# An encoder layer on one core: the up projection by 1024 columns with tokens stationary, its results transposed, and another order in the last down blocks

## The chip, the cores and the metric

The kernel runs on one core of a Trainium2 chip. The time of a version is the device time of one execution in microseconds, and the median over runs is compared. In the views PE is the matrix engine (PEld its weight loads), DVE the vector engine, ACT the scalar engine, POOL the GpSimd engine and SP the engine that issues most DMAs. A matmul has a stationary side (at most 128 x 128, loaded first) and a moving side (at most 512 columns), and adds up in one of eight PSUM banks of 128 x 512 numbers.

## The reference

256 tokens, model width 2048, inner width 8192, all in float32:

```python
h = rms_norm(x, norm_mix_pre)
proj = h @ w_in                     # q, k, v of two attentions, two gates
...
mixed = g_a * (oa @ w_branch_a) + g_b * (on @ w_branch_b)
x = x + rms_norm(mixed @ w_out, norm_mix_post)
h = rms_norm(x, norm_mlp_pre)
u = square(relu(h @ w_up))          # 2048 -> 8192
x = x + rms_norm(u @ w_down, norm_mlp_post)
```

## The kernel before

**Products.** Every float32 operand is split into a high part in the matrix engine's own 32-bit format and the rest. A product is then three matmuls: high by high, high by rest, rest by high. Splitting a weight costs an ACT cast (the high part) and a DVE subtraction (the rest). Weights come as 1 MB tiles on SP's queue, three buffers of each kind in the pool `wp`.

**Two ways to lay out a projection.** In `wgroup` (L184) the weight is stationary and the activations move: for each 128 rows and 128 columns one matmul of 512 moving columns (the high parts of the 256 tokens, then their rests, L192) and one of 256 (weight rest by high parts, L193). Results come out with columns on partitions. Their two halves are added in `halves` (L252). In `agroup` (L221) and `wide_group` (L671) the tokens are stationary, 128 at a time, and the weight moves, 512 columns in each matmul. `wide_group` works on 1024 columns of the weight and takes its rows in eight pairs of 128. One pair is a 2 x 2 by 2 x 2 block product of 128 x 128 and 128 x 512 blocks: eight products of blocks, 24 matmuls (`eight`, L656), or seven products by Winograd's scheme, 21 matmuls (`seven`, L644). Seven products need sums of weight blocks (`pair_weights`, L602, lines L612 to L623), sums of activation blocks (`sums_of`, L693), four more PSUM banks and a recombination of five vector steps (`combine`, L662).

**The stages.** (1) q, k, v and the attentions, (2) the gates and the branch projections with `wide_group`, (3) the output projection with `agroup` in four groups of 512 columns (L896), (4) the normalised residual, transposed and split into eight tiles `h2T` by `residual_parts(t, c)` (L849; t is the half of the tokens, c a quarter of the columns), (5) the up projection (L993), (6) the down projection (L1050), (7) the final norm, residual and stores (`finish`, L1036).

**Up projection.** Sixteen groups of 512 columns with `wgroup`. The per-token scale of the norm is broadcast along the tokens by two small matmuls (`along_tokens`). `u_evac` adds the halves, applies relu and the scale, and squares. `act_sets` (L947) then makes what the down projection needs of these 512 columns: for an even group number four sums of blocks and the splits of blocks and sums, for an odd one the splits alone. They are written to DRAM (POOL's queue, L974). Two groups' sets stay on the chip.

**Down projection.** Two halves of 1024 output columns (g), each in eight blocks of four row pairs (`steps`, L1054). The sets of the next block are fetched back by `act_again` (L979), with DMAs issued on ACT's queue (L987). In each block two of the four pairs use seven products, in the first block of a half one. In the last block the pairs go seven, eight, seven, eight; after the second seven the recombination runs, and in the last pair each bank is finished and handed to `down_piece` (L1027: addition, square with row sum, gain). `finish(t)` runs when both banks of a token half are done.

**Buffers and order.** Most tiles live in a pool of 27 buffers of 4 KB per partition (`pages`); a second, small pool `mid` of five such buffers holds the splits of the weight sums. Scratch tiles of stages 1 and 3 to 5 come from a pool `tmp`. Each engine's queue is laid out by the framework's own scheduler, which may put a ready instruction ahead of one that stands earlier in the program; `issue_after` forbids that for a single instruction.

Of the kernel before, what the change touches and what calls it, by code (L numbers as in the profile page):

```python
# [38 lines left out]
def encoder_layer(ctx: ExitStack, tc: tile.TileContext, a, out):  # L39
# [559 lines left out]
    def wtile(tag, name):  # L599
        return wp.tile([P, 4, 512], F32R, tag=tag, name=name)  # L600

    def pair_weights(view, name, seven):  # L602


        raw = wp.tile([P, 4, 512], F32, tag="raw", name=f"{name}r")
        last_load[0] = nc.sync.dma_start(raw.rearrange("p (h b) c -> p h (b c)", h=2), view).ins
        h1, l1 = wtile("hi", f"{name}h"), wtile("lo", f"{name}l")
        if not seven:
            nc.scalar.copy(h1, raw)
            nc.vector.tensor_sub(l1, raw, h1.bitcast(F32))  # L610
# [3 lines left out]
        nc.vector.tensor_add(t[0], raw[:, 1:3], raw[:, 0:1].to_broadcast([P, 2, 512]))  # L614
        nc.vector.tensor_add(t[1][:, 0], t[0][:, 0], raw[:, 2])
        nc.vector.tensor_add(t[1][:, 1], t[1][:, 0], raw[:, 3])
        nc.vector.tensor_sub(l1[:, 1:4], raw[:, 1:4], h1[:, 1:4].bitcast(F32))
        h2, l2 = [], []
        for i in range(2):
            for part, n in ((h2, "eh"), (l2, "el")):  # L620
                part.append(mid.tile([P, 2, 512], F32R, tag="e", name=f"{name}{n}{i}"))
            nc.scalar.copy(h2[i], t[i])
            nc.vector.tensor_sub(l2[i], t[i], h2[i].bitcast(F32))  # L623
        return h1, l1, h2, l2
# [3 lines left out]
    class Products:  # L628

        def __init__(self, name, mm_banks, used=range(8)):
            self.ps = {i: bank(f"{name}{i}", i in mm_banks) for i in used}
            self.begun = set()

        def add(self, i, stat, w, blk, last=False):

            (sh, sl), (wh, wl) = stat, w
            nc.tensor.matmul(self.ps[i], sh, wh[:, blk], start=i not in self.begun, stop=False)  # L639
            self.begun.add(i)  # L640
            nc.tensor.matmul(self.ps[i], sh, wl[:, blk], start=False, stop=False)  # L641
            nc.tensor.matmul(self.ps[i], sl, wh[:, blk], start=False, stop=last)  # L642

        def seven(self, stat, w, last):  # L644

# [22 lines left out]
            nc.vector.tensor_sub(c12, self.ps[4], c12)  # L668
            nc.vector.tensor_sub(c22, self.ps[4], c21)

    def wide_group(name, kinds, view, stat7, stat8, mm_banks, z, piece, each=None):  # L671


        any7 = any(s for _, s in kinds)
        pr = Products(name, mm_banks, range(8) if any7 else (1, 2, 3, 7))
# [17 lines left out]
    def sums_of(p1, p2, name, hi=None, lo=None):  # L693

        a11, a21, a12, a22 = p1[:, :P], p1[:, P:], p2[:, :P], p2[:, P:]
        s = t2k(f"{name}s").rearrange("p a (b c) -> p (a b) c", b=2)
# [55 lines left out]
    for h in range(2):  # L752
        gate = []
        for br, gc in (("a", GA), ("b", GB)):
# [30 lines left out]
            if first_one:  # L785
                advance(99)
                temps.close()
                stage = ctx.enter_context(ExitStack())
                mid = stage.enter_context(tc.tile_pool(name="mid", bufs=5, reuse_waits="tile"))
# [22 lines left out]
        mixed.append(gate[0])  # L812
    for n in range(2):
        mixed_T(1, n)
    stage.close()
    temps = ctx.enter_context(ExitStack())
    tmp = temps.enter_context(tc.tile_pool(name="tmp", bufs=6, reuse_waits="tile"))


    def mstat(k, t):  # L820
# [20 lines left out]
    r2b = const.tile([P, T], F32, name="r2b")  # L841
    hT2 = [page([P, 2, 512], F32R, f"h2T{i}") for i in range(8)]

    def post_norm(t):
# [38 lines left out]
    def mlp_squares(t):  # L883
        for c in range(4):
            cs = slice((c % 2) * 512, (c % 2 + 1) * 512)
            j = junk512("jx").rearrange("p a b -> p (a b)")
# [9 lines left out]
    for cg in range(4):  # L896

        def y_evac(t, ps, cg=cg):
            j = junk512("jy").rearrange("p a b -> p (a b)")
# [9 lines left out]
    mlp_squares(0)  # L909
    tail = [residual_parts(1, 0)]  # L910
    after = {1: tail[0][1:]}


    def first_up_inner(k):
        if k == 1:
            tail.append(residual_parts(1, 1, tail[0][2]))
            after[2] = tail[-1][1:]
            return tail[-1][0]

    def first_up_chunk(ch):  # L920
        if 1 <= ch <= 2:
            residual_parts(0, ch + 1)
            tail.append(residual_parts(1, ch + 1, tail[-1][2]))
        if ch == 2:
            with tc.issue_after(tail[-1][1]):
                mlp_squares(1)
            for t in range(2):
                mlp_scale(t)

    first_up = dict(  # L930
        after=after,
        hook=first_up_chunk,
        inner=first_up_inner,
        mid=partial(along_tokens, r2, r2b, "r2b"),
        k_first=True,
    )

# [52 lines left out]
        return out  # L990

    sets = {}
    for cg in range(NG):  # L993
        u = page([P, 4, T], F32, f"u{cg}")

        def u_evac(b, ps, u=u):
            s = halves(ps, "up")
            nc.vector.scalar_tensor_tensor(s, s, 0.0, r2b, op0=ALU.max, op1=ALU.mult)  # L998
# [8 lines left out]
    temps.close()  # L1007
    mid = ctx.enter_context(tc.tile_pool(name="mid2", bufs=5, reuse_waits="tile"))
    wd = a["w_down"].rearrange("(g h j p) c -> p h g j c", h=2, j=2, p=P)

    def dstat7(sets, j, n):
# [38 lines left out]
    for g in range(2):  # L1050
        pr = Products(f"p{g}", (1, 2, 3, 7))
        for bi, b in enumerate(blocks[g]):
            if bi == 0:
# [3 lines left out]
            end = bi == len(blocks[g]) - 1  # L1057
            for n, (cg, j, seven) in enumerate(steps):
                w = pair_weights(wd[:, :, cg, j, g * 1024 : (g + 1) * 1024], f"d{g}{cg}{j}", seven)
                if n == 0:  # L1060
                    for c in range(2):
                        if not end:
# [10 lines left out]
                if g == 1 and bi == 6:  # L1073
                    gain(0, n // 2, n % 2)
                if seven:
                    pr.seven(partial(dstat7, sets[g, cg], j), w, end and n == 2)
                    if end and n == 2:
# [65 lines left out]
```

## Time and profile before

| | |
|---|---|
| median of three runs | 1376.75 us (1376.13 to 1379.43) |
| profiled execution, device time | 1378.19 us |
| its span in the trace | 1376.4 us |
| up projection, first matmul to last | 663.8 to 1026.4 us |
| PE, DVE, ACT busy | 98%, 72%, 52% |
| mean granted PE clock | 0.993 |

The rows of the profile have the form: line, engine, operation, written tile <- read tiles, shapes, count, busy time, mean duration in ns, idle time before, and what ended it. In a timeline the first number is the start, the second the length; "x8" groups several instructions. Durations of matmuls overlap, so the time that one costs is read from the distances between starts.

### The profile page before, as it was taken

The numbers are of one execution on the slowest core, as the hardware profiler recorded it, in microseconds if no ns is written. First come the engines' busy times: TensorE is split into PE (matmuls) and PEld (weight loads), VectorE is DVE, ScalarE is ACT, GpSimd is POOL, SyncE is SP. The second block draws the span as 40 slices with busy tenths as digits, with TensorE's granted clock in tenths as the row PEclk, the third lists the DMA queues.
The fourth block names the chain that finished last, engine by engine and source line by source line (L and its number), as shares of the span: only waits on it lengthen the run. The fifth ranks groups of instructions, "written<-read, shape, count | busy, mean of one in ns | idle before, by whom it ended". The sixth has DMA issues, their size and how long they took to land.

```text
span 1376.4 us, 17243 instructions
## 1 busy us (share of the span) xinstructions
PE 1345.8 (98%) x6771; PEld 1141.3 (83%) x6771; DVE 997.7 (72%) x1245; ACT 709.7 (52%) x939; POOL 34.3 (2%) x67
## 2 busy tenths in 40 slices
PE   7999999999999999999899999999999999999995
PEld 6888888888888888888788888888887888888884
DVE  6868866677857886654767666666667888888886
ACT  7455555544644554444755555555554455555552
POOL 0000000000000000000000000000000000000000
PEclk9999999999999999999999999999999999999998
DMA  8684745564555665666477777877779989699982
GB/s 304 204 229 159 207 154 183 174 186 154 198 191 191 214 205 190 225 237 198 138 257 248 248 245 255 267 244 239 267 253 350 346 337 355 239 355 353 354 337 87
DMA packets 131633, 329.63 MB, mean 239 GB/s; under 512 B 17120, under 2 KB 18400, under 8 KB 131552
## 3 DMA queue, kind: packets, MB, share of 16 engines
q1 hardware_dynamic: 113168, 264.03, 57.5%
q10 hardware_dynamic: 12240, 40.91, 7.7%
q0 software_dynamic: 6144, 23.60, 4.2%
q8 instruction: 53, 0.87, 0.3%
q14 instruction: 28, 0.23, 0.0%
HBM read 302.81 MB, written 27.51 MB: 240 GB/s over the span
## 4 chain that ended last, share of the span: by engine, by line
PE 92%; DVE 3%; DMA 3%; ACT 1%; issue 1%; ACTq 0%; POOL 0%; SPq 0%; DVEq 0%; POOLq 0%
PE u_p L192 17%; PE u_p L193 9%; PE p L641 6%; PE p L642 6%; PE p L639 6%; PE qa_p L192 2%; PE ka_p L192 2%; PE qn_p L192 2%; PE kn_p L192 2%; PE ga L639 2%; PE y_p L232 2%; PE ga L641 2%; PE ga L642 2%; PE y_p L230 2%; PE y_p L231 2%; PE gb L639 2%
## 5 line engine op out<-in xcount | busy, mean ns | idle before, releaser
L192 PE MATMUL u_p<-h2T,u_h 128*128 128x512 f32 x1024 | 359.5, 397 | 1.0 <-DVE h2T L870 1.0
L193 PE MATMUL u_p<-h2T,u_l 128*128 128x256 f32 x1024 | 284.2, 280 | 0.0
L192 PEld LDWEIGHTS u_p<-h2T,u_h 128*128 128x128 f32 x1024 | 191.7, 188 | 45.8 <-DVE h2T L870 1.2
L117 DVE TENSOR_TENSOR u_l<-u_w,u_h 128x1024 fp32r<-128x1024 f32 x128 | 151.1, 1222 | 89.7 <-ACT u_h L116 88.4
L193 PEld LDWEIGHTS u_p<-h2T,u_l 128*128 128x128 f32 x1024 | 193.6, 189 | 1.3
L116 ACT CAST u_h<-u_w 128x1024 fp32r<-128x1024 f32 x128 | 128.0, 1048 | 94.0 <-PE u_p L192 83.5
L117 DVE TENSOR_TENSOR y_l<-y_w,y_h 128x1024 fp32r<-128x1024 f32 x32 | 37.9, 1222 | 30.9 <-ACT y_h L116 30.9
L116 ACT CAST y_h<-y_w 128x1024 fp32r<-128x1024 f32 x32 | 32.1, 1051 | 40.9 <-PE y_p L232 32.5
L230 PE MATMUL y_p<-y_h,mh 128*128 128x512 f32 x128 | 50.1, 391 | 0.0
L231 PE MATMUL y_p<-y_l,mh 128*128 128x512 f32 x128 | 49.9, 390 | 0.0
L232 PE MATMUL y_p<-y_h,ml 128*128 128x512 f32 x128 | 49.8, 390 | 0.0
L192 PE MATMUL qa_p<-hT,qa_h 128*128 128x512 f32 x128 | 47.7, 419 | 1.2 <-DVE hT L275 1.2
L192 PE MATMUL qn_p<-hT,qn_h 128*128 128x512 f32 x128 | 45.9, 400 | 0.0
L192 PE MATMUL kn_p<-hT,kn_h 128*128 128x512 f32 x128 | 45.4, 398 | 0.0
L192 PE MATMUL ka_p<-hT,ka_h 128*128 128x512 f32 x128 | 45.0, 398 | 0.0
L999 ACT ACTIVATE u<-up_s 128x256 f32<-128x256 f32 x64 | 24.8, 417 | 26.7 <-DVE up_s L998 26.7
L255 ACT COPY up_r<-u_p 128x256 f32<-128x256 f32 x64 | 23.6, 368 | 26.4 <-PE u_p L193 26.3
L193 PE MATMUL qn_p<-hT,qn_l 128*128 128x256 f32 x128 | 35.9, 281 | 0.0
L193 PE MATMUL kn_p<-hT,kn_l 128*128 128x256 f32 x128 | 35.7, 280 | 0.0
L193 PE MATMUL qa_p<-hT,qa_l 128*128 128x256 f32 x128 | 35.2, 285 | 0.0
L193 PE MATMUL ka_p<-hT,ka_l 128*128 128x256 f32 x128 | 35.2, 280 | 0.0
L192 PEld LDWEIGHTS qa_p<-hT,qa_h 128*128 128x128 f32 x128 | 24.9, 197 | 6.7 <-DVE hT L275 1.6
(1397 smaller groups left out, 3449.6 us busy)
## 6 DMA issues: line engine op xcount, KB each, us to landing
u_w<-in_w_up SPq DMA_DIRECT2D x64, 1024.0 KB, 5.6
y_w<-in_w_out SPq DMA_DIRECT2D x16, 1024.0 KB, 5.3
bh<-keeph ACTq DMA_DIRECT2D x30, 512.0 KB, 10.0
bl<-keepl ACTq DMA_DIRECT2D x30, 512.0 KB, 11.7
keeph<-ah POOLq DMA_DIRECT2D x18, 512.0 KB, 3.9
keepl<-al POOLq DMA_DIRECT2D x18, 512.0 KB, 3.9
ka_w<-in_w_in SPq DMA_DIRECT2D x8, 1024.0 KB, 6.7
va_w<-in_w_in SPq DMA_DIRECT2D x8, 1024.0 KB, 5.1
```

The source lines that it names most:

```text
L116: nc.scalar.copy(hi[part], raw[part])
L117: nc.vector.tensor_sub(lo[part], raw[part], hi[part].bitcast(F32))
L192: nc.tensor.matmul(ps[b], hi[:, k % 4, cs], mv, start=(k == 0), stop=False)
L193: nc.tensor.matmul(ps[b][:, :T], lo[:, k % 4, cs], mv[:, :T], start=False, stop=(k == nk - 1))
L230: nc.tensor.matmul(ps[t], sh, hi[:, k % 4], start=(k == 0), stop=False)
L231: nc.tensor.matmul(ps[t], sh, lo[:, k % 4], start=False, stop=False)
L232: nc.tensor.matmul(ps[t], sl, hi[:, k % 4], start=False, stop=(k == nk - 1))
L255: nc.scalar.copy(r, ps[:, T:])
L639: nc.tensor.matmul(self.ps[i], sh, wh[:, blk], start=i not in self.begun, stop=False)
L641: nc.tensor.matmul(self.ps[i], sh, wl[:, blk], start=False, stop=False)
L642: nc.tensor.matmul(self.ps[i], sl, wh[:, blk], start=False, stop=last)
L999: nc.scalar.activation(u[:, b], s, AF.Square)
```

## The change

1. **Up projection.** The sixteen `wgroup` calls become eight calls of `wide_group` with 1024 columns each, eight row pairs in each call. In the first call all pairs use eight products; in the other seven, pairs 3 and 5 use seven. The activation sums for these two pairs are made at the end of the first call. `u_piece` adds the recombined part where there is one, and applies relu and the per-token scale, which now lies along partitions; the broadcast over tokens goes. `u_sets` transposes 512 columns of the result by eight matrix-engine transposes into two PSUM banks, ACT squares them into `u`, and `act_sets` follows as before. It runs for group g during pairs 1 and 2 of group g + 1; for the last group during the first block of the down projection.
2. **The first call's order.** For its first two row pairs, the products of token half 0 come first for both pairs, then `residual_parts(1, 0)`, then those of token half 1. The other residual parts follow at pairs 2 to 4, the squares and scales of both halves at pair 5.
3. **Down projection.** The last block of each half goes eight, seven, eight, eight, with its matmuls issued in program order (`in_order`). The second split part of the weight sums (`l2`) comes from the pool of 27 instead of `mid`.
4. **Buffers.** PSUM banks of a `wide_group` are taken when first used. The pool `tmp` isn't opened again after stage 2, `mid` stays open, and the scratch tiles of stages 3 to 5 and of `sums_of` come from the pool of 27.

```diff
-    def pair_weights(view, name, seven):
+    def pair_weights(view, name, seven, low=None):
...
+                if low and part is l2:
+                    part.append(low(shape, F32R, n))
+                else:
+                    part.append(mid.tile(shape, F32R, tag="e", name=n))
...
         def add(self, i, stat, w, blk, last=False):
             (sh, sl), (wh, wl) = stat, w
-            nc.tensor.matmul(self.ps[i], sh, wh[:, blk], start=i not in self.begun, stop=False)
-            self.begun.add(i)
-            nc.tensor.matmul(self.ps[i], sh, wl[:, blk], start=False, stop=False)
-            nc.tensor.matmul(self.ps[i], sl, wh[:, blk], start=False, stop=last)
+            if i not in self.ps:
+                self.ps[i] = bank(f"{self.name}{i}", i in self.mm_banks)
+            for n, (st, mv) in enumerate(((sh, wh), (sh, wl), (sl, wh))):
+                with tc.issue_after(self.after) if self.after else nullcontext():
+                    ins = nc.tensor.matmul(
+                        self.ps[i], st, mv[:, blk], start=i not in self.begun, stop=last and n == 2
+                    ).ins
+                self.begun.add(i)
+                self.after = ins if self.in_order else None
...
+            if turn and n < 2:
+                ahead = [*ahead, (i, w)] if n else [(i, w)]
+                for t in range(2) if n else ():
+                    for ii, ww in ahead:
+                        for which in (2 * t, 2 * t + 1):
+                            pr.eight(partial(stat8, ii), ww, which, False)
+                    if not t:
+                        turn()
+                continue
...
+    def first_up(n):
+        for t, c in {2: [(1, 1), (0, 2)], 3: [(1, 2), (0, 3)], 4: [(1, 3)]}.get(n, ()):
+            residual_parts(t, c)
+        if n == 5:
             for t in range(2):
+                mlp_squares(t)
                 mlp_scale(t)
...
-        def u_evac(b, ps, u=u):
-            s = halves(ps, "up")
-            nc.vector.scalar_tensor_tensor(s, s, 0.0, r2b, op0=ALU.max, op1=ALU.mult)
-            nc.scalar.activation(u[:, b], s, AF.Square)
-
-        wgroup(a["w_up"], cg * 512, lambda k: hT2[k // 2][:, k % 2], KD, u_evac, f"u{cg}", **({} if cg else first_up))
+        for b in range(2):
+            pt = bank(f"uT{cg}{b}")
+            for j in range(2):
+                for t in range(2):
+                    c = (b * 2 + j) * P
+                    nc.tensor.transpose(
+                        pt[:, j * T + t * P : j * T + (t + 1) * P], z[t][:, cg % 2, c : c + P], ident
+                    )
+            nc.scalar.activation(
+                u[:, b * 2 : b * 2 + 2], pt.rearrange("p (j q) -> p j q", j=2), AF.Square
+            )
         got = act_sets(cg, u)
...
+    def u_piece(t, half, ps, summed, z):
+        zt = z[t][:, half]
+        if summed:
+            nc.vector.tensor_add(zt, zt, ps)
+        nc.scalar.activation(zt, zt if summed else ps, AF.Relu, scale=r2[:, t : t + 1])
+
+    UPS = [(0, 0), (1, 0), (2, 0), (3, 1), (4, 0), (5, 1), (6, 0), (7, 0)]
+    uz = None
+    for g in range(DFF // 1024):
+        z = [page([P, 2, 512], F32, f"u{g}{t}") for t in range(2)]
...
+        def up_each(n, g=g, uz=uz):
+            if not g:
+                first_up(n)
+                if n == 7:
+                    for i in (3, 5):
+                        f = page([P, 2, T], F32, f"h2f{i}")
...
+                        h2sum[i] = sums_of(f[:, 0], f[:, 1], f"h2s{i}")
+            elif n in (1, 2):
+                u_sets(g * 2 - 3 + n, uz)
+
+        wide_group(
+            f"u{g}",
+            UPS if g else ALL8,
...
+            turn=None if g else partial(residual_parts, 1, 0),
+        )
+        uz = z
...
+            elif end:
+                steps = [(b + 1, 0, 0), (b, 0, 1), (b, 1, 0), (b + 1, 1, 0)]
+                pr.in_order = True
...
-                w = pair_weights(wd[:, :, cg, j, g * 1024 : (g + 1) * 1024], f"d{g}{cg}{j}", seven)
+                w = pair_weights(wd[:, :, cg, j, g * 1024 : (g + 1) * 1024], f"d{g}{cg}{j}", seven, page)
+                if g == 0 and bi == 0 and n in (1, 2):
+                    u_sets(NG - 3 + n, uz)
```

More of the change, by code (lines that the diff above doesn't have):

```diff
@@ L620, in pair_weights @@
             for part, n in ((h2, "eh"), (l2, "el")):
-                part.append(mid.tile([P, 2, 512], F32R, tag="e", name=f"{name}{n}{i}"))
+                shape, n = [P, 2, 512], f"{name}{n}{i}"
+                if low and part is l2:
+                    part.append(low(shape, F32R, n))
+                else:
+                    part.append(mid.tile(shape, F32R, tag="e", name=n))
             nc.scalar.copy(h2[i], t[i])
@@ L628, in encoder_layer, with __init__ @@
     class Products:
-        def __init__(self, name, mm_banks, used=range(8)):
-            self.ps = {i: bank(f"{name}{i}", i in mm_banks) for i in used}
+        def __init__(self, name, mm_banks):
+            self.name, self.mm_banks = name, mm_banks
+            self.ps = {}
             self.begun = set()
+            self.in_order, self.after = False, None
         def add(self, i, stat, w, blk, last=False):
             (sh, sl), (wh, wl) = stat, w
-            nc.tensor.matmul(self.ps[i], sh, wh[:, blk], start=i not in self.begun, stop=False)
-            self.begun.add(i)
-            nc.tensor.matmul(self.ps[i], sh, wl[:, blk], start=False, stop=False)
-            nc.tensor.matmul(self.ps[i], sl, wh[:, blk], start=False, stop=last)
+            if i not in self.ps:
[7 more added lines that the diff above has]
+                self.after = ins if self.in_order else None
         def seven(self, stat, w, last):
@@ L669, in combine, with wide_group @@
             nc.vector.tensor_sub(c22, self.ps[4], c21)
-    def wide_group(name, kinds, view, stat7, stat8, mm_banks, z, piece, each=None):
+    def wide_group(name, kinds, view, stat7, stat8, mm_banks, z, piece, each=None, turn=None):
         any7 = any(s for _, s in kinds)
-        pr = Products(name, mm_banks, range(8) if any7 else (1, 2, 3, 7))
+        pr = Products(name, mm_banks)
         for n, (i, seven) in enumerate(kinds):
@@ L1004, in encoder_layer @@
             sets[0, cg] = got
-    temps.close()
-    mid = ctx.enter_context(tc.tile_pool(name="mid2", bufs=5, reuse_waits="tile"))
+    def u_piece(t, half, ps, summed, z):
[13 more added lines that the diff above has]
+                        f = page([P, 2, T], F32, f"h2f{i}")
+                        for k in range(2):
+                            d = hT2[i][:, k].bitcast(F32)
+                            nc.vector.tensor_add(f[:, k], d[:, :T], d[:, T:])
+                        h2sum[i] = sums_of(f[:, 0], f[:, 1], f"h2s{i}")
[4 more added lines that the diff above has]
+            UPS if g else ALL8,
+            lambda i, c=g * 1024: a["w_up"][i * T : (i + 1) * T, c : c + 1024].rearrange(
+                "(k p) c -> p k c", p=P
+            ),
+            h2stat7,
+            h2stat8,
+            (1, 2, 3, 7),
+            z,
+            partial(u_piece, z=z),
+            each=up_each,
+            turn=None if g else partial(residual_parts, 1, 0),
+        )
+        uz = z
     wd = a["w_down"].rearrange("(g h j p) c -> p h g j c", h=2, j=2, p=P)
@@ L1075, in encoder_layer @@
                 if seven:
-                    pr.seven(partial(dstat7, sets[g, cg], j), w, end and n == 2)
-                    if end and n == 2:
+                    pr.seven(partial(dstat7, sets[g, cg], j), w, end)
+                    if end:
                         for t in range(2):
```

49 lines of the change are left out of this document (15 added, 34 removed).

## The prediction

> **What bounds the kernel now.** I read the page's first part, then the matrix engine's waits, then the rows of the stages that the change touches.
>
> ```profile
> span 1376.4 us, 17243 instructions
> PE 1345.8 (98%) x6771; PEld 1141.3 (83%) x6771; DVE 997.7 (72%) x1245; ACT 709.7 (52%) x939; POOL 34.3 (2%) x67
> ```
>
> ```profile
> PE h2T_t L860 <- DVE x L853: 3.2, 1, 3.2
> PE p L639 <- ACT d000eh L622: 2.5, 1, 2.5
> PE u_p L192 <- DVE h2T L870: 1.0, 1, 1.0
> PE p L639 <- DVE zw L1029: 0.6, 1, 0.6
> ```
>
> PE is busy for 98% of the span and waits a few microseconds at stage borders. So the time is PE's list of products, plus these waits, plus what follows the last product. A change pays if it makes the list shorter or closes a border. What the other engines gain or lose counts only where PE waits for them.
>
> The time of one product is the distance between starts, since durations overlap. The up projection, first and last start:
>
> ```profile
> L192 PE MATMUL u_p<-h2T,u_h x1024: 387/395/796, 663.8 to 1026.1; 128*128 128x512 f32 x171
> L193 PE MATMUL u_p<-h2T,u_l x1024: 274/280/415, 664.4 to 1026.4; 128*128 128x256 f32 x171
> ```
>
> Two stretches give the prices: the middle of that stage, counting L192 alone (us, PE busy and count, weight loads, clock, DMA), and the middle of the down projection, where every product is 512 wide (us, PE, weight loads, DVE, ACT, POOL, clock, DMA):
>
> ```profile
> 700.00:1000.00 300.00, 299.03 (x858) 159.91 (x857) 1.00 0.76 254
> ```
>
> ```profile
> 1070.00:1160.00 90.00, 90.00 (x399) 74.55 (x398) 76.15 (x63) 46.06 (x35) 0.00 (x0) 1.00 0.90 350
> ```
>
> Adding one duration for the instruction cut by the edge, a pair of one 512-wide and one 256-wide product takes (300 + 0.4)/858 = 0.350 us, and a 512-wide product (90 + 0.4)/399 = 0.2265. The 256-wide one therefore costs 0.1235, which is 0.0103 more than half of a 512-wide one.
>
> **The exchange of shapes, and the seven products.** Now there are 1024 pairs: 1024 x 0.350 = 358.4 us. Afterwards the tokens are the stationary side: 8 groups x 8 row pairs x 24 products = 1536, all 512 wide, 1536 x 0.2265 = 347.9. The columns streamed are equal (1024 x 768 = 1536 x 512); the surplus of the narrow product goes: -10.5. In 14 of the 64 row pairs 24 products become 21: 42 x 0.2265 = -9.5. What is left is 338.4.
>
> The Trainium skill (TensorE: Matmul & The Clock Gate, "Back-to-back issue gap") gives a warm product as N/2.4 + 2.5 ns, 109 ns at 256 and 216 at 512. By it the exchange saves only 512 x 2.5 ns = 1.3 us (an estimate from that page). The trace disagrees: 123.5 ns against 226.5, more than half.
>
> **The transposes that are added.** Each 512 columns of the result are transposed by 8 instructions, 128 in all. The kernel has such transposes already, in front of a branch projection:
>
> ```profile
> 523.42 0.39 PE L642 MATMUL gb<-gb_7h,hT 128*128 128x512 f32 x1
> 523.65 1.03 PE L741 MATMUL mT<-ident,ga 128*128 128x128 f32 x8
> 524.44 0.48 PE L639 MATMUL ba<-ba_0h,oaT 128*128 128x512 f32 x1
> 524.76 0.40 PE L641 MATMUL ba<-ba_0l,oaT 128*128 128x512 f32 x1
> ```
>
> From 523.42 to 524.76 lie two products and 8 transposes: (1.34 - 0.453)/8 = 0.111 us each. 128 x 0.111 = +14.2, of which 16 (1.8 us) fall into the first down block.
>
> ```profile
> L741 PE MATMUL mT<-ident,ga x32: 270/272/273, 523.7 to 577.2; 128*128 128x128 f32 x32
> ```
>
> ```profile
> 520.00:580.00 60.00, 60.00 (x282) 49.98 (x281) 37.04 (x35) 25.47 (x26) 0.00 (x0) 1.00 0.56 183
> ```
>
> One transpose lasts 272 ns, and the clock stayed at 1.00 in the 60 us that hold all 32. The Trainium skill (TensorE: Matmul & The Clock Gate, "PE-mode transpose") warns of about 275 ns in a kernel's context and says that a transpose does not count as activity for the clock. The duration agrees; the distance between starts and the clock do not bear out a price of that size.
>
> **The border into the up projection.** Last product of the output projection, first of the up projection, and the stretch around it:
>
> ```profile
> 658.55 0.40 PE L232 MATMUL y_p<-y_h,ml 128*128 128x512 f32 x1
> ```
>
> ```profile
> 663.77 0.80 PE L192 MATMUL u_p<-h2T,u_h 128*128 128x512 f32 x1 [1.00 <-DVE h2T L870]
> ```
>
> ```profile
> 660.00:680.00 20.00, 16.89 (x94) 14.79 (x95) 17.17 (x35) 14.59 (x33) 1.09 (x2) 0.91 0.50 158
> ```
>
> From 658.78 (658.55 + 0.2265) to 1026.5 (1026.4 + 0.1235) are 367.7 us. Less 358.4 of pairs, 24 transposes of the second residual (L860, at 0.111: 2.7) and the two small products of the row scale (some 0.3, priced like transposes), 6.3 is lost: 4.2 us of waits (the L860 and L192 rows) and about 20 x 0.09 = 1.8 of lowered clock. Every product now needs both token halves, and the second half's normalisation ends at 663.8. Afterwards the first two row pairs do their 24 products of the first token half first: 24 x 0.2265 = 5.4 us, until 664.2, after that chain's end. What may stay is that the second pair's split (one 2.29 us DVE subtraction, row below) now lies beside the same chain: between 0 and some 4 us, as DVE goes in order. I keep 2.0, nearer to the one subtraction. So the stage costs 338.4 + 2.7 + 14.2 + 2.0 = 357.3, against 367.7: **-10.4**.
>
> **Who hides the new vector work.** DVE loses the two 256-wide steps of each 128 columns and gains the sums of a seven pair, the recombination and four additions per group. The middle of the up stage, all engines (columns as above), and the two steps that go:
>
> ```profile
> 700.00:1000.00 300.00, 300.00 (x1715) 261.34 (x1714) 196.09 (x264) 161.57 (x240) 20.93 (x39) 1.00 0.76 254
> ```
>
> ```profile
> L998 DVE SCALAR_TENSOR_TENSOR up_s<-up_s,r2b 128x256 f32<-128x256 f32 x64 | 25.4, 421 | 1.0
> L257 DVE TENSOR_TENSOR up_s<-u_p,up_r 128x256 f32<-128x256 f32 x64 | 25.2, 418 | 0.0
> ```
>
> A seven pair on DVE, from the down projection:
>
> ```profile
> 1168.81 1.22 DVE L614 TENSOR_TENSOR d0140t<-d0140r 128x1024 f32<-128x1024 f32 x1
> 1169.95 1.75 DVE L617 TENSOR_TENSOR d0140l<-d0140r,d0140h 128x1536 fp32r<-128x1536 f32 x1
> 1171.62 0.68 DVE L615 TENSOR_TENSOR d0140t<-d0140t,d0140r 128x512 f32<-128x512 f32 x1
> 1172.22 1.22 DVE L623 TENSOR_TENSOR d0140el<-d0140t,d0140eh 128x1024 fp32r<-128x1024 f32 x1
> 1173.35 0.68 DVE L616 TENSOR_TENSOR d0140t<-d0140t,d0140r 128x512 f32<-128x512 f32 x1
> 1173.96 2.29 DVE L610 TENSOR_TENSOR d0150l<-d0150r,d0150h 128x2048 fp32r<-128x2048 f32 x1
> ```
>
> By distances a seven pair takes 5.15 plus a second L623 of 1.13, 6.3 us, against 2.2 for a plain one. Per 1 MB row pair DVE now has 196.09 x 5.6/300 = 3.66 us. Less 50.6/64 = 0.8, plus 2/8 x 4.1 = 1.0, plus eight steps of 0.6 over eight pairs = 0.6, that is 4.5 us in a pair of 357/65 = 5.5: 82%. The down row has DVE at 76.15 of 90 us with PE at 90.00, so this cover holds, and ACT gets less. I take 0. Without cover a seven pair could come late by its excess of 4.1 us. The loads stay 1 MB per pair on SP's queue, and the stores of the results stay on POOL's queue, each behind its split.
>
> **The border into the down projection.**
>
> ```profile
> 1045.86 0.39 PE L642 MATMUL p<-d0120eh,al 128*128 128x512 f32 x1
> 1048.78 0.83 PE L639 MATMUL p<-d000eh,bh 128*128 128x512 f32 x2 [2.53 <-ACT d000eh L622]
> ```
>
> ```profile
> 1047.31 0.33 ACTq L987 DMA_DIRECT2D bl<-keepl  x1
> 1047.68 1.99 ACT L622 CAST d000eh<-d000t 128x1024 fp32r<-128x1024 f32 x2 [6.27 <-DMA bl<-keepl]
> ```
>
> ```profile
> 1040.00:1060.00 20.00, 17.47 (x70) 13.81 (x69) 13.53 (x12) 7.73 (x7) 0.00 (x0) 0.91 1.03 404
> ```
>
> A reload (L987) sat at the head of ACT's queue until 1047.31, and the cast that PE needed lay behind it: 2.92 - 0.23 = 2.7 us, and 1.8 of lowered clock, 4.5 together. The change moves the last two result sets into this first block, nine buffers more at the moment when the reload wants some. It also takes one of the two split parts of the sums out of the small pool. Bounds: the stall goes (-4.5), or there are two of it (+4.5). I take 0, as the reload's place is unchanged.
>
> **The last blocks and the end.** One seven pair in each becomes plain: 6 x 0.2265 = +1.4. Their products go in written order, so a late split can no longer be jumped over: 0 to 2 us each, +1.0 together. The wait of 0.6 before the second half (L639 on L1029) goes, as its first bank is now free 4 us earlier: -0.6. Then the end:
>
> ```profile
> 1358.58 0.69 DVE L666 TENSOR_TENSOR zw<-zw,p 128x512 f32<-128x512 f32 x1 [5.59 <-PE p L642]
> ```
>
> ```profile
> 1359.90 0.61 PE L642 MATMUL p<-d1131h,bl 128*128 128x512 f32 x2
> ```
>
> ```profile
> 1366.57 2.74 DVE L1043 SCALAR_TENSOR_TENSOR zw<-zw,rd_r,x 128x512 f32<-128x512 f32 x4 [0.39 <-POOL rd_r L89]
> 1369.22 0.15 DVE L86 TENSOR_SCALAR rd_m<-sd 128x1 f32<-128x1 f32 x1
> 1370.10 2.74 DVE L1043 SCALAR_TENSOR_TENSOR zw<-zw,rd_r,x 128x512 f32<-128x512 f32 x4 [0.72 <-POOL rd_r L89]
> ```
>
> ```profile
> L1032 ACT ACTIVATE jd<-zw 128x512 f32<-128x512 f32 x8 | 5.0, 624 | 11.5 <-DVE zw L1029 11.5
> ```
>
> PE ends at 1360.5 and the span at 1376.4: 15.9 us, filled by DVE, which begins the recombination only 1.9 us before PE's end. Afterwards 48 products (10.9 us) follow the seven pair, so the recombination lies under them, and the banks close one after another, 6 products (1.36 us) apart. After the last product remain one addition (0.69), one square (0.62 and its sum, some 0.8), reduction and scale (0.35), 0.88 from L86 to L1043, 2.74, and 3.56 from 1372.84 to the span's end: 9.1. If the first half's four L1043 lie in front, as they do in these rows, up to 2.4 more. I take 10.5: **-5.4**.
>
> **Sum:** -10.4 + 0 + 1.4 + 1.0 - 0.6 - 5.4 = -14.0. Span 1376.4 to 1362.4; the profiled run's 1378.19 to 1364.2. That run lies 1.4 above the median of the three, 1376.75, from which I forecast 1362.8.
>
> **Rivals.** A: the stall at the down border goes too, since the other half of the sums' parts leaves the small pool; against it, nine more buffers: 1358.3. B: the order of the queues doesn't come out as written; the first token half fills nothing (6.3 stays, +4.3) and half of the end's gain is lost (+2.7): 1369.8. C, slower: the pool of 27 buffers. At a group's second pair it must hold 8 of activations, 4 of the residual, 2 of sums, 4 of two groups' results and 9 of the sets, 27 in all, and the next seven pair wants two more, which come free when a store lands:
>
> ```profile
> keeph<-ah POOLq DMA_DIRECT2D x18, 512.0 KB, 3.9
> ```
>
> If each of the 14 seven pairs comes 1.5 us late for it, +21: 1383.8; it decides from 1.0 us each. Against it: results of the group before come free in the same pair. D: the narrow product's surplus is no matter of shape and stays in another form: +10.5, 1373.3. That is the case of the skill's gap formula above. E: a transpose costs PE its 272 ns: 128 x 0.161 = +20.6, 1383.4; the four rows speak against it. The skill's sentence on transposes stands behind this one.
>
> **Chances.** Forecast 0.56, A 0.14, B 0.12, C 0.09 (a third of it mild, within 0.3%), D 0.05, E 0.04. A measurement here can tell about 0.3%, 4.1 us: faster is under 1372.6, slower over 1380.9. Faster 0.56 + 0.14 + 0.12 = 0.82; same 0.05 + 0.03 = 0.08; slower 0.06 + 0.04 = 0.10. The range 1354 to 1374 reaches below A by the end's and the border's lower bounds (about 4) and above to D; C and E, 0.13, and the tails of the others stay out.
>
> **What would show it.** Right: up products 512 wide at 0.2265, about 1494; first of them before 660; 128 transposes at 0.111; seven pairs without PE waits; recombination done before the last product; some 10.5 us after it. Wrong: PE waits on casts or sums in the up stage, L974's stores or L987's reloads ahead of them, or a clock under 1.00 behind the transposes.

## The result, and the profile after

| | before | after |
|---|---|---|
| median | 1376.47 us (1376.13 to 1379.43, 4 runs) | 1367.81 us (1367.57 to 1368.72, 4 runs) |
| profiled execution, its span | 1378.19 / 1376.4 us | 1367.94 / 1366.2 us |

The ratio is 0.9934, with a 95% interval of 0.9918 to 0.9949: the changed kernel is 8.7 us faster, where 14.0 were forecast; 1367.81 lies in the range. The median of before has a fourth run in it now. Between the two traces the gain is 10.2 us, since the profiled run of before lay 1.7 us above its median and that of after 0.1. The steps below are held against the 10.2.

The first part of the page of after:

```profile
span 1366.2 us, 16268 instructions
PE 1340.7 (98%) x6347; PEld 1119.4 (82%) x6347; DVE 1034.7 (76%) x1181; ACT 717.8 (53%) x843; POOL 33.9 (2%) x67
```

PE has 424 matmuls fewer, DVE has 37 us more to do, and PE is again busy for 98%: still a kernel of one list of products. The list itself first, by the transposes' row and a stretch in which every instruction is a 512-wide product or one of the 128 transposes (us, PE busy and count, weight loads, DVE, ACT, POOL, clock, DMA):

```profile
L1009 PE MATMUL uT<-ident,u x128: 270/272/273, 711.2 to 1029.2; 128*128 128x128 f32 x128
```

```profile
700.00:1030.00 330.00, 330.00 (x1519) 273.58 (x1518) 264.46 (x253) 195.32 (x190) 23.02 (x43) 1.00 0.74 261
```

With the prediction's prices, (1519 - 128) x 0.2265 + 128 x 0.111 = 329.3 of the 330.4 us (330 and the last one's overhang). So prices and counts hold but for 1.1 us. These are no waits: products that don't stand next to a transpose start 0.2272 us apart there on average, instead of 0.2265, and no two of them more than 0.24. Why, stays open. DVE is at 80% (264 of 330).

Then the list of what PE waited for, after:

```profile
PE p L649 <- DMA bh<-keeph: 1.6, 3, 0.9
PE u L649 <- DVE ry_m L86: 1.1, 1, 1.1
PE u L649 <- ACT h2T L885: 0.9, 1, 0.9
PE p L649 <- ACT d001eh L626: 0.8, 2, 0.6
PE p L649 <- DVE d011l L610: 0.6, 1, 0.6
```

The waits of before on the whole second half (h2T_t on x, 3.2) and on zw are gone. New are reloads (keeph) and, still, the activations h2T. To see all of what PE loses, not only named waits, I add up the distances between starts of products and subtract 0.2265 (0.111 for a transpose) for each. After: 3.3 us from 640 to 680, 1.1 in the rest of the up stage, 6.4 between 1040 and 1080, nothing in the last blocks. A second trace of the same kernel gives 3.3, 1.1, 6.5 and nothing. Before, by the same account: 6.2, 0.1, 4.5, and 1.6 in the last blocks.

**The border into the up projection**, PE and then DVE:

```profile
658.52 0.40 PE L232 MATMUL y_p<-y_h,ml 128*128 128x512 f32 x1
658.76 0.39 PE L649 MATMUL u<-u_0h,h2T 128*128 128x512 f32 x1
...
661.75 0.50 PE L649 MATMUL u<-u_0h,h2T 128*128 128x512 f32 x1 [0.88 <-ACT h2T L885]
...
664.08 0.72 PE L649 MATMUL u<-u_0h,h2T 128*128 128x512 f32 x2 [1.12 <-DVE ry_m L86]
```

```profile
657.54 2.29 DVE L610 TENSOR_TENSOR u_1l<-u_1r,u_1h 128x2048 fp32r<-128x2048 f32 x1
659.74 1.12 DVE L886 SCALAR_TENSOR_TENSOR h2T<-h2T_t,g_mlp,h2T 128x128 fp32r<-128x128 f32 x4
...
661.47 2.29 DVE L610 TENSOR_TENSOR u_2l<-u_2r,u_2h 128x2048 fp32r<-128x2048 f32 x1
663.67 0.35 DVE L886 SCALAR_TENSOR_TENSOR h2T<-h2T_t,g_mlp,h2T 128x128 fp32r<-128x128 f32 x1
```

The up projection starts 0.24 us after the last product of the stage before, where it took 5.2 (658.55 to 663.77). It then has three short waits. The releaser of the last is named as the scale in L86, but the product at 664.08 starts right behind the L886 that ends at 664.02: that step makes h2T and sat behind the 2.29 us subtraction of pair 2, as the group at 659.74 sat behind that of pair 1.

**The border into the down projection** (columns as above), and ACT:

```profile
1040.00:1060.00 20.00, 18.50 (x76) 13.56 (x75) 15.30 (x13) 9.89 (x10) 1.06 (x2) 1.00 0.77 298
1060.00:1080.00 20.00, 17.92 (x76) 13.55 (x75) 18.34 (x15) 12.05 (x10) 0.00 (x0) 1.00 1.00 388
```

```profile
1047.72 1.04 ACT L626 CAST d000eh<-d000t 128x1024 fp32r<-128x1024 f32 x1
1052.51 1.05 ACT L626 CAST d000eh<-d000t 128x1024 fp32r<-128x1024 f32 x1 [3.75 <-DVE d000t L616]
1052.52 0.39 ACTq L984 DMA_DIRECT2D bh<-keeph  x1
...
1054.91 0.48 ACTq L984 DMA_DIRECT2D bl<-keepl  x1
```

A stretch of 20 us without a wait (1080 to 1100) counts 90 products, with those that its edges cut; here it is 76 in each of the two. It is no longer one stall of 2.5 us, and the clock stays at 1.00: it is many waits of 0.2 to 0.9. Six reloads leave ACT's queue in one go at 1052.5 to 1055.4, behind a cast that waited 3.75 us for a weight sum; PE needs them from 1057 on. Of the 6.4 us, 4.7 are lost between 1057 and 1066, where the DMA engines are full (1.00, 388 GB/s). Weights come late there too: the casts of d020 at 1055.5 and of d030 at 1059.4 waited 1.9 and 2.4 us for their transfers.

**The end**, PE, DVE and SP:

```profile
1353.79 0.39 PE L649 MATMUL p<-d1131h,bl 128*128 128x512 f32 x1
```

```profile
1344.82 0.68 DVE L680 TENSOR_TENSOR zw<-p,zw 128x512 f32<-128x512 f32 x1
...
1354.21 0.69 DVE L1080 TENSOR_TENSOR zw<-zw,p 128x512 f32<-128x512 f32 x1
...
1356.37 2.73 DVE L1094 SCALAR_TENSOR_TENSOR zw<-zw,rd_r,x 128x512 f32<-128x512 f32 x4
1359.02 0.14 DVE L86 TENSOR_SCALAR rd_m<-sd 128x1 f32<-128x1 f32 x1
1359.88 2.74 DVE L1094 SCALAR_TENSOR_TENSOR zw<-zw,rd_r,x 128x512 f32<-128x512 f32 x4 [0.72 <-POOL rd_r L89]
```

```profile
1357.14 5.84 SPq L1097 DMA_DIRECT2D out_y<-zw  x8
```

The recombination (its last step is L680) is done at 1345.5, before the last product, as foreseen; PE ends at 1354.2, the span at 1366.2: 12.0 us instead of 15.9.

### The profile page after: what moved, and what is told of

It reads as the page before. It is cut to its first block, busy times and chain, and to the rows that moved or that the text cites. A ratio compares the mean times of both kernels' runs of the same rounds, so it can differ in the third digit from the quotient of the medians.

```text
span 1366.2 us, 16268 instructions
## 1 busy us (share of the span) xinstructions
PE 1340.7 (98%) x6347; PEld 1119.4 (82%) x6347; DVE 1034.7 (76%) x1181; ACT 717.8 (53%) x843; POOL 33.9 (2%) x67
## 4 chain that ended last, share of the span: by engine, by line
PE 96%; DVE 1%; DMA 1%; issue 0%; ACT 0%; ACTq 0%; SPq 0%; DVEq 0%; POOLq 0%; POOL 0%
PE u L649 25%; PE p L649 23%; PE ga L649 6%; PE gb L649 6%; PE ba L649 3%; PE bb L649 3%; PE qa_p L192 2%; PE ka_p L192 2%; PE qn_p L192 2%; PE kn_p L192 2%; PE y_p L230 2%; PE y_p L231 2%; PE y_p L232 2%; PE qa_p L193 1%; PE qn_p L193 1%; PE kn_p L193 1%
## 5 line engine op out<-in xcount | busy, mean ns | idle before, releaser
L649 PE MATMUL u<-u_0h,h2T 128*128 128x512 f32 x128 | 44.6, 392 | 2.3 <-DVE ry_m L86 1.1
L649 PE MATMUL u<-u_1h,h2T 128*128 128x512 f32 x128 | 44.6, 396 | 0.0
L649 PE MATMUL u<-u_4h,h2T 128*128 128x512 f32 x128 | 42.1, 390 | 0.0
L649 PE MATMUL u<-u_2h,h2T 128*128 128x512 f32 x128 | 41.8, 397 | 0.0
L649 PE MATMUL u<-u_6h,h2T 128*128 128x512 f32 x128 | 41.8, 389 | 0.0
L649 PE MATMUL u<-u_7h,h2T 128*128 128x512 f32 x128 | 41.0, 389 | 0.0
L609 ACT CAST u_1h<-u_1r 128x2048 fp32r<-128x2048 f32 x8 | 15.3, 1913 | 36.1 <-PE u L649 32.6
L649 PEld LDWEIGHTS u<-u_0h,h2T 128*128 128x128 f32 x128 | 23.9, 188 | 8.4 <-DVE ry_m L86 1.6
```

The source lines that it names most:

```text
L649: ins = nc.tensor.matmul(self.ps[i], st, mv[:, blk], start=i not in self.begun, stop=last and n == 2).ins
```

## The experiments

All ratios are to the kernel before, measured on the same chip, with 95% intervals; the changed kernel has 0.9934, and measured again beside three of the experiments (7, 9 and 10) 0.9937 (0.9925 to 0.9950). "Lost" is the account of starts above.

**1. No seven products in the up projection.**

```diff
-    UPS = [(0, 0), (1, 0), (2, 0), (3, 1), (4, 0), (5, 1), (6, 0), (7, 0)]
+    UPS = ALL8
```

> The changed kernel with eight products in all 64 row pairs of the up projection. Theory (the time is the matrix engine's list of products plus the waits at stage borders plus the end): 42 products of 0.2265 us come back, so 9.5 us slower than the changed kernel, about 1377.3 us; no matrix-engine wait inside the up stage with or without them. Rival (the sums and their buffers cost part of what the shorter list gains, in the up stage or at the down border): clearly less than 9.5, at most 6, and the loss at the down border shrinks.

1378.43 us, 1.0003 (0.9994 to 1.0012): 9 to 9.5 us slower than the changed kernel. The 42 products are worth their full 9.5; no time was being lost to the sums. The rival also asked for a smaller loss at the down border, and it was 7.8 us here instead of 6.4.

**2. The transposes twice.** Each of the 128 is issued twice into the same place, so PE has 128 more instructions and the result is unchanged.

```diff
-            for j in range(2):
-                for t in range(2):
+            for j, t in 2 * [(j, t) for j in range(2) for t in range(2)]:
...
```

> The changed kernel with every one of the 128 added transposes done twice, into the same place. Theory: 128 x 0.111 = 14.2 us slower, about 1382, clock 1.00. Rival (a transpose costs its duration of 272 ns, or lowers the clock): 20 to 35 us slower, 1388 to 1403. A second rival (transposes fill gaps): under 7 us.

1380.85 us, 1.0024 (1.0015 to 1.0033): 12.4 slower by the ratios, 14.4 by the spans (the profiled run lay 1.5 above its median). The stretch that holds them, as above:

```profile
700.00:1040.00 340.00, 338.50 (x1608) 282.47 (x1607) 262.54 (x247) 191.95 (x185) 22.68 (x42) 1.00 0.72 251
```

128 x 0.111 = 14.2; rival E falls (at 272 ns each it would be 34.8), and the clock is 1.00 with twice as many transposes. By the distances between starts the 256 take 0.110 us each.

**3. The old last blocks in the changed kernel**, and **4. the new last blocks alone in the kernel before.** The edit of 3 (4 is the reverse, put into the old kernel):

```diff
-            elif end:
-                steps = [(b + 1, 0, 0), (b, 0, 1), (b, 1, 0), (b + 1, 1, 0)]
-                pr.in_order = True
...
-                    pr.seven(partial(dstat7, sets[g, cg], j), w, end)
-                    if end:
+                    pr.seven(partial(dstat7, sets[g, cg], j), w, end and n == 2)
+                    if end and n == 2:
```

> The changed kernel with the last block of each half as before: pairs seven, eight, seven, eight, and the scheduler's own order of matmuls. Theory: 6 products fewer (-1.4), but the recombination lies at the end again: 15.9 us after the last product instead of 12.0 (+3.9), and a small wait at the start of the second half (+0.6): about 3 us slower, 1371. Rival (the list order itself costs, so the end's gain is eaten before the last product): no difference, 1367 to 1368.

> The kernel before with the new order of the last down blocks alone (eight, seven, eight, eight, matmuls in program order). Theory: +1.4 for 6 products, -3.9 at the end, -0.6 at the second half's start: about 3 us faster than before, 1373.4. Rival (the end is shorter only because the rest of the change leaves the vector engine less behind): within 1 us of before.

The old blocks: 1371.02 us, 0.9959 (0.9945 to 0.9972), some 3.4 slower. The new ones alone: 1374.14 us, 0.9971 (0.9961 to 0.9982), 4 faster than before. In 3 the recombination again runs behind the last product:

```profile
1352.65 0.39 PE L649 MATMUL p<-d1131h,bl 128*128 128x512 f32 x1
```

```profile
1353.86 0.68 DVE L680 TENSOR_TENSOR zw<-p,zw 128x512 f32<-128x512 f32 x1
```

From PE's end there are 16.2 us to the end of the span, and 12.0 in experiment 4. The sum for 4: -3.9 at the end, -1.6 of waits in the last blocks, +1.4 for six products, that is -4.1.

**5. Without the order by token halves.** The framework's scheduler gets the products pair by pair.

```diff
-            turn=None if g else partial(residual_parts, 1, 0),
+            turn=None,
...
+                if n == 0:
+                    residual_parts(1, 0)
```

> The changed kernel without the first group's order: the first residual part of the second token half stands ahead of all up products, and each pair does both halves before the next pair. Theory: the border into the up projection loses some 6 us again instead of 2.5, about 3.5 to 4 slower than the changed kernel, 1371.5. Rival (the scheduler finds the products of the first half by itself): same within 1 us.

1368.73 us, 0.9935 (0.9922 to 0.9949): there is no difference to the changed kernel. The border in this run:

```profile
659.03 0.40 PE L232 MATMUL y_p<-y_h,ml 128*128 128x512 f32 x1
659.27 0.39 PE L649 MATMUL u<-u_0h,h2T 128*128 128x512 f32 x1
...
664.59 0.73 PE L649 MATMUL u<-u_0h,h2T 128*128 128x512 f32 x2 [1.12 <-DVE ry_m L86]
```

It lost 3.3 us from 640 to 680, as both traces of the changed kernel did, wait for wait. The theory was wrong: the order written in the program is worth nothing that shows, and the scheduler puts the products of the first half first by itself. What is left as the reason is that the tokens are stationary, so that such products exist at all; no run tests that alone.

**6. Last two sets kept on the chip: blocks reordered so that the first down block needs no reload.**

```diff
-    FIRST = (NG - 4, NG - 2)
+    FIRST = (NG - 6, NG - 4, NG - 2)
...
-    blocks = [[NG - 4] + list(range(0, NG - 4, 2)) + [NG - 2], [NG - 2] + list(range(0, NG - 2, 2))]
+    LAST = NG - 6
+    blocks = [[NG - 4, NG - 2] + list(range(0, LAST + 1, 2)), [LAST] + list(range(0, LAST, 2)) + [NG - 4, NG - 2]]
...
```

> The changed kernel with another order of down blocks: the first half takes columns' blocks 12, 14, 0, 2, 4, 6, 8, 10 and the second 10, 0, 2, 4, 6, 8, 12, 14, so that the sets of the last two groups stay on the chip for the second block and no reload is wanted until the third. The stored results grow by the one block product that an eight-product pair of block 10 needs. Theory (the down border loses some 8 us because reloads wait for buffers that the last two sets hold): the loss falls to 0 to 2, so 6 to 8 us faster than the changed kernel, about 1360.5. Rival (the border is slow because vector and scalar engine have the two sets to make there besides the weights): no more than 2 us faster.

1368.49 us, 0.9938 (0.9926 to 0.9951): no gain. The waits on reloads are gone, and others came in their place:

```profile
PE p L649 <- DVE d0120el L627: 2.4, 1, 2.4
```

```profile
1032.80 1.22 DVE L968 TENSOR_TENSOR al<-sm,ah 128x1024 fp32r<-128x1024 f32 x1
1033.93 1.22 DVE L614 TENSOR_TENSOR d0120t<-d0120r 128x1024 f32<-128x1024 f32 x1
...
1039.08 1.22 DVE L627 TENSOR_TENSOR d0120el<-d0120t,d0120eh 128x1024 fp32r<-128x1024 f32 x1
```

The subtraction of this pair's other part (L617) had been done at 1020.62, so its weights were there. Its sums stand on DVE behind parts of the last two result sets (the L968 is one). So to take the reloads away gains nothing here: the sums of a seven pair and the last result sets share DVE's queue. But it isn't the wait of the changed kernel. There the same sums come nearly as late (the two L627 start at 1037.54 and 1040.48, here at 1039.08 and 1042.01), and PE loses nothing to them, as it has products of the second block to do meanwhile. This run has put the last two groups in that block's place, and PE runs out of products at 1037.6. In the changed kernel the late sums are those of the second block's first seven pair (d000t, for which ACT waited the 3.75 us above); that the reloads behind them cost nothing isn't shown.

**7. The seven pair later.** First down block eight, eight, eight, seven, the middle blocks eight, seven, eight, seven.

```diff
-                steps = [(b + 1, 0, 0), (b, 1, 0), (b, 0, 1), (b + 1, 1, 0)]
+                steps = [(b + 1, 0, 0), (b, 1, 0), (b + 1, 1, 0), (b, 0, 1)]
...
-                steps = [(b, 0, 1), (b + 1, 0, 0), (b, 1, 1), (b + 1, 1, 0)]
+                steps = [(b + 1, 0, 0), (b, 0, 1), (b + 1, 1, 0), (b, 1, 1)]
```

> The changed kernel with the seven-product pair last in the first down block, and the middle blocks of both halves in the order eight, seven, eight, seven. The number of products is the same. Theory (formed on the run that held the sets: the border is slow because the sums of the first seven-product pair stand behind the last two sets on the vector engine's queue, which wait for transposes that wait for the end of the up projection; nothing needs those sums until three plain pairs are done): the loss at the border falls from 6.4 to 2 or less, 4 to 5 us faster than the changed kernel. Rival (buffers: the pool of 27 is full whatever the order): within 1.5 us of the changed kernel.

1368.22 us, 0.9936 (0.9923 to 0.9948). The border fell from 6.4 to 2.3 us, as the theory of DVE's queue says. The reloads also left earlier, at 1041.5 instead of 1052.5, as ACT no longer waited for sums in front of them, so late sums and late reloads aren't told apart. Full DMA engines alone aren't the cause: they are as full here (1.02 and 1.03 from 1040 to 1080). The gain was given back at the ends of the two halves, 2.2 us each:

```profile
PE p L649 <- DVE d1120el L627: 1.9, 1, 1.9
PE p L649 <- DVE d0140el L627: 1.9, 1, 1.9
```

The last block begins with a plain pair and its seven pair; since the block before now ends with a seven pair as well, two seven pairs have one plain pair between them, and in written order PE can't jump over the late one.

**8. The second part of the sums back in the small pool**, and **9. with 7 together.**

```diff
-... f"d{g}{cg}{j}", seven, page)
+... f"d{g}{cg}{j}", seven)
```

> The changed kernel with the second split part of the weight sums back in the small pool of five buffers in the down projection. If the pool of 27 is what runs out at the down border: 2 to 6 us faster there, and no loss in the middle, where the kernel before had no waits. If the small pool is what holds the vector engine back: slower, with matrix-engine waits on casts and subtractions of sums.

> The run before with the second split part of the weight sums in the small pool again. If order was the cause and the pool a part of it, both gains add up in part: 4 to 7 us faster than the changed kernel. If both act on the same wait: no faster than the better of the two. If two sevens in a row of plain pairs need the room: slower than the run before.

8: 1366.47 us, 0.9921 (0.9909 to 0.9933), the lowest time of all versions; the border lost 3.6 us. Its interval overlaps that of the changed kernel, so a gain of 1.8 is likely but not certain, and experiment 11 weakens it. 9: 1372.67 us, 0.9961 (0.9949 to 0.9974), some 3.3 slower than the changed kernel. A wait of 1.9 us on a weight cast is new, and that cast waited for its weight's transfer. That five small buffers are too few with the seven pairs late is a guess that no row shows. The two edits don't add up; of the three outcomes expected, the last one (slower than the run before) came.

**10. Scale of the second half earlier**, on top of 9. `finish` is cut in two; the second half's reduction and scale come before three of the first half's four last steps, and the first half's scale ahead of the last addition.

```diff
...
+                        with tc.issue_after(scales[0][1]) if g and which == 3 else nullcontext():
+                            down_piece(g, t, half, pr.ps[bank_])
...
+                            scales.append(scale_of(which // 2))
+                        if g and which == 3:
+                            for i in range(2):
+                                finish(i, scales[i][0], scales[1][1])
```

> The run before with the end's vector work in another order: the first token half's scale stands ahead of the last bank's addition, and the second half's scale ahead of three of the first half's four last steps. Theory (12.0 us after the last product are a chain on the vector engine in which the second scale waits for the first half's steps): 10.0 to 10.5 after the last product, about 2 us faster than the run before. Rival (the store of the last part sets the end): under 0.5.

1372.74 us, 0.9966 (0.9954 to 0.9978), as 9 (0.9961). From PE's end to the end of the span 11.8 us instead of 12.0:

```profile
1359.89 0.68 DVE L1081 TENSOR_TENSOR zw<-zw,p 128x512 f32<-128x512 f32 x1
1360.66 0.75 DVE L1102 SCALAR_TENSOR_TENSOR zw<-zw,rd_r,x 128x512 f32<-128x512 f32 x1
...
1362.23 4.71 DVE L1102 SCALAR_TENSOR_TENSOR zw<-zw,rd_r,x 128x512 f32<-128x512 f32 x7
```

The pause of 0.7 us in front of the second half's steps is gone, yet the last addition came later for its new place (0.8 us behind PE's end), and the end hardly moved, as the rival says.

**11. Small pool and another end.** As 8; of 10 the split and the order of the last steps, not the order of the addition; the second half's gains on GpSimd, its stores from ACT's queue.

```diff
...
-        nc.vector.tensor_mul(z, z, gp2...
+        (nc.gpsimd if g and t else nc.vector).tensor_mul(z, z, gp2...
...
-            nc.sync.dma_start(out...
+            (nc.scalar if t else nc.sync).dma_start(out...
```

> The changed kernel with the second part of the weight sums back in the small pool (as in the run that had this alone and came to 1366.47 us, 0.9921), and with another end: the gains of the second token half go to GpSimd, the scale of the second half stands ahead of three of the first half's four last steps, and the second half's stores leave from ACT's queue instead of SP's. Theory: the 12.0 us behind the last product are a chain of some 13 vector steps on DVE (8.4 us), then 3.6 us until the last store has landed. Two steps of about 0.6 us leave that chain, the stores no longer stand eight in one queue: about 10.5 us behind the last product, about 1364.9 us, some 1.5 us faster than the run with the small pool alone. Rival: GpSimd's steps are slow or slow DVE down, or the landing of a store sets the end whatever the queue: 12 us or more behind the last product, no gain (1366.5 us or above).

1368.15 us, 0.9933 (0.9919 to 0.9946): the rival. PE ended at 1354.2, the span at 1366.4: 12.2 us. The rows are of DVE and of GpSimd; then come the DMA engines between 1355 and 1367 in 40 slices of 0.3 us:

```profile
1356.27 1.75 DVE L1102 SCALAR_TENSOR_TENSOR zw<-zw,rd_r,x 128x512 f32<-128x512 f32 x1 [0.17 <-POOL rd_r L1094]
```

```profile
1356.21 1.25 POOL L1077 TENSOR_TENSOR zw<-zw,gp 128x512 f32<-128x512 f32 x1
```

```profile
DMA  0000000000000999999999999999999740000000
```

```profile
DMA packets 1152, 2.10 MB, mean 175 GB/s; under 512 B 128, under 2 KB 128, under 8 KB 1152
```

The first of the eight last steps started 0.06 us behind GpSimd's gain and took 1.75 us, where such a step took 0.75 in experiment 10: what DVE no longer did itself, it waited for. The Trainium skill (SBUF — State Buffer, "SBUF: two separate sides") says that a vector step with two operands in SBUF and a GpSimd step that reads SBUF exclude each other for a whole instruction; the trace agrees, for this one step: it ends at 1358.02, 0.56 us behind GpSimd's.

The stores keep the DMA engines full from 1358.9 until about 1364.5, whichever queue issues them: 2.10 MB in 5.6 us. So from the first store's issue (1358.04) to the end there are 0.9 until data moves, 5.6 of transfer and 1.9 behind it, 8.4 together. In the changed kernel the same sum from 1357.14 gives 1365.5 of its 1366.2; the rest is the pause before the second half. In experiment 10 it gives 1369.8 of 1370.9, from a first store at 1361.44: that store left 0.6 us sooner behind PE's end than in 9, but DMA then stood still until the second one. So what counts by these traces is when the first store leaves and whether the next ones follow without a pause. A version in which the whole row of stores leaves earlier wasn't tried.

The border of 11, whose program there is that of 8, lost 5.9 us where 8 lost 3.6. The stretch from 1060 to 1080, of 8 and then of 11:

```profile
1060.00:1080.00 20.00, 18.29 (x80) 14.58 (x79) 16.21 (x14) 9.85 (x8) 0.00 (x0) 1.00 0.91 340
```

```profile
1060.00:1080.00 20.00, 17.69 (x71) 13.96 (x70) 15.42 (x13) 9.62 (x7) 0.00 (x0) 0.91 0.89 347
```

The same order of instructions met a weight 0.9 us later and a clock of 0.91. So one trace of that version fixes this border only to some 2.4 us, and the small pool's part in it stays open: 8 and 11 together lie at about 0.9927, 1 us below the changed kernel.

## Why the prediction was right, and where it was off

**Right in its main sum.** The exchange of shapes (-10.5), the seven products (-9.5) and the transposes (+14.2) came as priced: the stretch 700 to 1030 is accounted for to 1.1 of 330 us, experiment 1 measured 9 to 9.5 for the seven products, experiment 2 12.4 to 14.4 for 128 transposes. Rivals D and E fall with this, and rival C with the up stage, where PE waits for nothing from 680 us on. Rivals A and B fall at the borders: the down border loses 6.4 us, not 0, and the up border 3.3, not 6.3. That DVE's added work is hidden held at 80% of load. One reading of a source was off: the formula behind rival D is given in the Trainium skill (TensorE: Matmul & The Clock Gate, "Back-to-back issue gap") for a single matmul by itself, and for a stream it has about 131 ns at 512 columns. The 226.5 ns of the trace agree with neither.

The 3.8 us between -14.0 and -10.2 are five terms:

- **Border into the up projection, +1.3.** Kept at 2.0, measured 3.3. The mechanism was named, a 2.29 us subtraction beside the chain, but two stood in it (pairs 1 and 2), not one. And the reason given for the gain was partly wrong: the order by halves need not be written (experiment 5).
- **Up stage, +1.1.** Taken as 0. It is not missing cover, as PE waits for nothing there: the products start 0.7 ns further apart than priced. The cause stays open.
- **Border into the down projection, +1.9.** Taken as unchanged, 4.5; it was 6.4, inside the bounds of 0 to 9. The reason, that the reload's place is unchanged, failed: the stall that was seen before (a cast behind a reload) went, and now the third block's reloads stand behind a cast that waits for late sums on DVE, where the last two result sets have their place too. Experiment 7 fits this; it doesn't part the sums from the reloads. Four traces with this border (after, its repeat, experiments 3 and 5) lost 6.4 to 6.7; that of before lost 4.5 and, in experiment 4, 3.4. So the term is some 2 to 3 us.
- **Last blocks, -2.0.** The sum had +1.0 for products in written order and -0.6 for the bank, +0.4 together. Instead no wait at all is left, where before 1.6 were lost. Experiment 4 carries this.
- **End, +1.5.** 10.5 us were forecast, 12.0 measured. The prediction counted DVE's chain (its terms add up to 9.0, not 9.1) and let the first half's four steps overlap by half. They lay in front entirely, and behind the first store 2.1 MB need 5.6 us, which the sum did not hold as a bound.

The last 1.5 us, from -10.2 to -8.7, are the profiled run of before, which lay above its median.

## What to carry to other kernels

Price an exchange of matmul shapes by distances between starts in a stretch where PE waits for nothing: here that held to a third of a per cent, while the larger errors came from the borders, where an engine's queue has work of two stages in it, and from the end. Look there for what else stands in the queue ahead of the step that PE needs, and not only for the transfer that shows up as late. A wait that was moved away came back at another place (experiments 6, 7 and 9). At the end, count the output's bytes behind the first store (5.6 us here) beside the chain of vector steps.

## What the runs showed of the hardware

A float32 128 x 128 transpose lasts 272 ns but takes 111 ns of PE's time in a stream of products, and 256 of them in 340 us left the granted clock at 1.00. Eight stores of 256 KB move at 2.10 MB in 5.6 us, 375 GB/s, from one queue or from two. A vector step with two operands in SBUF that began just behind a GpSimd step took 1.75 us instead of 0.75 (seen once).
